# A hybrid decoder step on one core: the opening's products without the token's factor, six row tiles, shared decays

## The chip, the core and the metric

The kernel runs on one core of a Trainium2 chip. TensorE (PE) multiplies matrices into accumulators in PSUM; VectorE (DVE), ScalarE (ACT) and GpSimd (POOL) work on tiles of up to 128 partitions in SBUF, and VectorE and ScalarE also read the accumulators; SyncE (SP) issues most loads. The metric is device time in microseconds of one execution, as the median of several runs.

## What is computed

One inference step of a decoder layer for a prompt of 512 tokens and for 8 sequences of 8 sample tokens, 576 tokens in all, width 1024. The part that the change touches is the layer's input side:

```python
sh1, sc1, g1, sh2, sc2, g2 = split(silu(c) @ ada_w + ada_b, 6)      # per sequence and feature
hn = rmsnorm(x, norm1_w) * (1 + sc1) + sh1                          # rmsnorm: x * rsqrt(mean(x*x) + eps) * w
u = hn @ w_in                                                       # z, xbc, dt, q, k, v, o, ig, fg, xr, gr
xbc = silu(causal_conv(xbc, ...))                                   # width 4, with a state for the samples
y, ssm = ssd_chunked(xs, dt, a, bm, cm, s0)                         # decay = exp(cum[t] - cum[s]), masked
```

Behind it come an mLSTM and an RG-LRU on other columns of `u`, the output projection, and an MLP. The token's factor is the rsqrt: one number per token, the same for all features.

## The kernel before

Features lie on partitions, in 8 tiles (`KT`) of 128; tokens lie along the free axis, 512 of the prompt (`TP`) and 64 of the samples (`TS`), in two halves of 288 (`HALF`). A product block is 128 columns of a weight by 1024 features. Weights and activations are each split into a high and a low part in a reduced type (`w_prep`: ScalarE copies `wh`, L150, VectorE subtracts for `wl`, L151), and `mm_k` (L163) does three products by two halves, 6 matmuls for a feature tile, 48 for a block. A block accumulates in a pair of PSUM banks `g`; the pool behind `PG` has two such pairs, so a block's first matmul waits until the block before the last one has been copied out.

The opening, `start`, is written in the order in which each engine runs it (`in_order`). SyncE issues 8 loads of `x`, a vector of constants, and 8 column groups of `ada_w` (`ada`, 4 loads each, L354) with weight blocks between. The squares of `x` are summed over features by TensorE (`ms`, L271), raised to -1/2 on GpSimd (`rstd_cols`), and spread over partitions by transposes and a copy (`rstd_bcast`, tile `rb`). For each feature tile k, a column group of `ada_w` gives shift and scale: `ada_mm` (L217, row copy L219) and `ada_sel` (two transposes L227, a reduction L229 and an addition L231 on VectorE). `modulate` makes the tile's normalised `hnh` and `hnl` from `x`, `rb` and the scale `amp` (L292 to L303). The products of blocks 1 to 3 follow tile by tile, a step after their tile is there; `warm` puts filling matmuls between.

Blocks 1, 2 and 3 belong to the convolutions 8, 10 and 0. After them come the gates' products (`gates_mm`, L430, on the normalised `x`), and then block 4 and all later ones through `unit`, which issues a block's products, evicts, and calls `slot` twice; each `slot` advances the generators that run beside (gate rows, SSD, mLSTM, LRU, the later ada groups) by a step.

A convolution's eviction (`ev_conv`, `conv`) uses two row tiles of a ring, `R`, of 4: rows `r` and the sum `a`. GpSimd fills the left edges (L610, L611), ScalarE copies the accumulator in three pieces (L612, L614, L615) and starts the sum (L621), VectorE adds three taps (L627), ScalarE takes a tanh (L650), and VectorE makes `xbc` (L652, L654). The SSD's generator prepares a chunk's operands in `front` (the decay E: four Relu steps, L710, then an Exp, on each half of the heads) and uses them in `back`.

Of the kernel before, what the change touches and what calls it, by code (L numbers as in the profile page):

```python
# [22 lines left out]
FT = mybir.dt.float32  # L23
FR = mybir.dt.float32r
# [7 lines left out]
NT = TP + TS  # L32
# [35 lines left out]
class Kernel:  # L68
# [24 lines left out]
    def R(self):  # L93
        return self.rpool.tile([128, 608], FT, name=self.name("r"), tag="r")
# [27 lines left out]
    def w_load(self, upto):  # L122
        while self.w_next_dma <= min(upto, NBLK - 1):
            b = self.w_next_dma
            t = self.T("wg") if b == 0 else self.wpool.tile([128, 1024], FT, name=self.name("raw"), tag="raw", bufs=RAW_BUFS)
            src = self.io["wg"] if b == 0 else self.io["w"][b - 1]
            n = src.shape[1]
            self.nc.sync.dma_start(t[:, :n], src)
            self.w_raw[b] = t[:, :n].rearrange("p (k m) -> p k m", k=8)
            self.w_next_dma += 1  # L130

# [155 lines left out]
    def modulate(self, x, rb, k):  # L287

        nc = self.nc
        amp = self.rpool.tile([128, 9], FT, name=self.name("amp"), tag="amp", bufs=3)  # L290
        sc, sh = self.mod("sc1", k), self.mod("sh1", k)
        nc.vector.tensor_scalar(amp, sc, 1.0, self.v("nw1")[:, k:k + 1], op0=OP.add, op1=OP.mult)  # L292
        p, s = x[:, :TP], x[:, TP:].rearrange("p (b t) -> p b t", b=NB)
        nc.vector.scalar_tensor_tensor(p, p, amp[:, 0:1], rb[:, :TP], op0=OP.mult, op1=OP.mult)
        nc.gpsimd.tensor_tensor(x[:, TP:], x[:, TP:], rb[:, TP:], op=OP.mult)
        nc.gpsimd.tensor_tensor(s, s, amp[:, 1:, None].to_broadcast([128, NB, 8]), op=OP.mult)
        nc.gpsimd.tensor_tensor(s, s, sh[:, 1:, None].to_broadcast([128, NB, 8]), op=OP.add)
        hi, lo = self.T("hnh", FR), self.T("hnl", FR)
        nc.scalar.activation(hi[:, :TP], p, AF.Identity, bias=sh[:, 0:1])
        nc.scalar.activation(hi[:, TP:], x[:, TP:], AF.Copy)  # L300
        nc.vector.scalar_tensor_tensor(lo[:, :TP], p, sh[:, 0:1], hi[:, :TP].bitcast(FT), op0=OP.add, op1=OP.subtract)  # L301
        nc.gpsimd.tensor_tensor(lo[:, TP:], x[:, TP:], hi[:, TP:].bitcast(FT), op=OP.subtract)
        nc.gpsimd.tensor_scalar(p, p, sh[:, 0:1], None, op0=OP.add)  # L303
        return hi, lo
# [24 lines left out]
    def start(self):  # L329
# [6 lines left out]
        with self.in_order():  # L336
            x = [self.T("x") for _ in range(KT)]
            for k in range(KT):
                nc.sync.dma_start(x[k], io["x"][:, k])
# [10 lines left out]

            def load(q):
                ada[q] = [self.T("ada") for _ in range(4)]
                for i in range(4):
                    nc.sync.dma_start(ada[q][i][:, :512], io["ada"][q, :, i * 512:(i + 1) * 512])  # L354

            for q in range(PAIR_AT):
                load(q)
                self.w_load(W_AT.get(q, 0))
            ms = self.P("ms")
            self.warm(WARM[0])  # L360
            for k in range(0, KT, 2):
                sa, sb = self.R()[:, :NT], self.R()[:, :NT]
                nc.scalar.activation(sa, x[k], AF.Square)
                if k:
                    nc.vector.tensor_tensor(sb, x[k + 1], x[k + 1], op=OP.mult)
                else:
                    nc.scalar.activation(sb, x[k + 1], AF.Square)
                nc.vector.tensor_tensor(sb, sa, sb, op=OP.add)
                self.sum_tokens(sb, ms, k == 0, k == KT - 2)
                if k < KT - 2:  # L370
                    self.warm(WARM[1])
            th = self.rpool.tile([128, 8, 32], FT, name="cth", tag="r")
# [3 lines left out]
            rows = {}  # L376

            def ada_mm(q):
                t = ada.pop(q)
                rows[q] = self.ada_mm(lambda k: t[k // 2][:, (k % 2) * 256:(k % 2 + 1) * 256])  # L380

            ada_mm(0)
            self.w_prep(0)
            for q in range(PAIR_AT, KT):
                if q == VEC_AT:
                    nc.sync.dma_start(self.vec[:, NV1:], io["vec"][:, NV1:])
                load(q)
                self.w_load(W_AT.get(q, 0))
            self.w_load(4)
            self.start_dma = self.last()  # L390
            rb = self.rstd_bcast(r)
            self.warm(WARM[2])
            self.ada_sel(0, rows[0])
            self.hn = [None] * KT
            self.hn[0] = self.modulate(x[0], rb, 0)
            self.w_prep(1)
            self.warm(WARM[3])
            ada_mm(1)
            self.ada_sel(1, rows[1])
            ada_mm(2)  # L400
            pgs = [self.PG(), self.PG(), PairTile(banks=[self.P("g"), self.P("g")])]
            for k in range(KT):
                if k + 1 < KT:
                    self.hn[k + 1] = self.modulate(x[k + 1], rb, k + 1)
# [1252 lines left out]
```

## Time and profile before

| | us |
|---|---|
| median of 3 runs (lowest, highest) | 977.28 (972.36, 979.8) |
| the profiled execution | 978.69 |
| its span, from the first to the last instruction | 976.9 |
| block 4's first matmul starts | 62.08 |
| block 5's, block 6's | 70.09, 76.44 |

The span is some 2 us shorter than the time of the same execution, since the time has the launch in it. In the page and in the answers of the trace a row of a group gives line, engine, operation, out<-in with the program's names, shape and number, then busy time and the mean of one in ns, then the engine's idle time before them and what ended it. A timeline's row gives start, duration, engine, line and tile, and in brackets the idle time before it and who ended it; a pair of halves is one row.

### The profile page before, as it was taken

To read this page: it belongs to the slowest core of one execution; us is meant where nothing else is said; L and a number is where in the kernel's file an instruction comes from. 1 tells how busy PE (TensorE), PEld (TensorE's weight loads), DVE (VectorE), ACT (ScalarE), POOL (GpSimd) and SP (SyncE) were. 2 spreads that over 40 slices of the span, in tenths; PEclk is the share of its full clock that TensorE was granted. 3 is DMA by queue.
4 is the path that set the end of the run, shared out by engine and by line. 5 is a ranking of instruction groups with operands and counts; after the bars stand their busy time and mean duration, and the time that the engine had idled before them with its cause. 6 is when DMAs were issued, how large, how long until landed. Compare 5 with 4: busy or idle time off the path is not lost.

```text
span 976.9 us, 18063 instructions
## 1 busy us (share of the span) xinstructions
PE 952.2 (97%) x7322; PEld 897.4 (92%) x7322; DVE 572.0 (59%) x1166; ACT 417.4 (43%) x805; POOL 136.8 (14%) x194
## 2 busy tenths in 40 slices
PE   8999899999999899999999999999999999999996
PEld 4689888888888899998999999999999999999996
DVE  3769887686885594666444456433553355335544
ACT  3356786485765664554222244312331243114321
POOL 1821213302441221110000000000000000000032
PEclk8999999999999999999999999999999999999998
DMA  9712275656633435333333222222222222222202
GB/s 345 302 66 87 76 209 179 228 164 189 219 130 122 153 110 176 120 128 124 111 111 109 80 87 86 71 82 88 87 87 74 79 87 87 87 77 76 87 23 97
DMA packets 51218, 119.61 MB, mean 122 GB/s; under 512 B 6956, under 2 KB 17468, under 8 KB 51136
## 3 DMA queue, kind: packets, MB, share of 16 engines
q1 hardware_dynamic: 47024, 111.06, 33.5%
q10 hardware_dynamic: 3744, 6.85, 1.8%
q8 instruction: 58, 0.95, 0.4%
q0 software_dynamic: 368, 0.55, 0.2%
q14 instruction: 24, 0.20, 0.1%
HBM read 108.68 MB, written 9.76 MB: 121 GB/s over the span
## 4 chain that ended last, share of the span: by engine, by line
PE 86%; DVE 3%; ACT 2%; DMA 1%; issue 1%; SPq 0%; POOL 0%; POOLq 0%; ACTq 0%; DVEq 0%
PE g L163 75%; PE adap L217 1%; PE g L1382 1%; DMA cumb<-scr_cum 1%; PE ps L742 1%; PE py L737 1%; PE pc L840 1%; PE lg L1148 1%; PE py L740 1%; DMA ada<-ada 1%; PE pu L847 0%; ACT att L710 0%; PE pu L997 0%; PE pn L989 0%; DVE wl L151 0%
## 5 line engine op out<-in xcount | busy, mean ns | idle before, releaser
L150 ACT ACTIVATE wh<-raw 128x1024 fp32r<-128x1024 f32 x123 | 130.0, 1058 | 348.1 <-PE g L163 326.9
L151 DVE TENSOR_TENSOR wl<-raw,wh 128x1024 fp32r<-128x1024 f32 x123 | 152.2, 1238 | 48.2 <-ACT wh L150 42.3
L163 PE MATMUL g<-hnh,wh 128*128 128x288 f32 x688 | 155.0, 305 | 8.8 <-ACT r L615 5.2
L163 PE MATMUL g<-hnh,wl 128*128 128x288 f32 x688 | 153.3, 302 | 0.3 <-DVE wl L151 0.3
L163 PE MATMUL g<-hnl,wh 128*128 128x288 f32 x688 | 151.5, 299 | 0.2 <-DVE hnl L301 0.2
L163 PEld LDWEIGHTS g<-hnh,wh 128*128 128x128 f32 x688 | 111.7, 190 | 17.4 <-ACT r L615 6.1
L163 PEld LDWEIGHTS g<-hnh,wl 128*128 128x128 f32 x688 | 111.7, 190 | 4.3 <-issue 3.1
L163 PEld LDWEIGHTS g<-hnl,wh 128*128 128x128 f32 x688 | 112.1, 190 | 2.6 <-issue 1.6
L163 PE MATMUL g<-h2h,wh 128*128 128x288 f32 (+1 forms) x512 | 111.2, 298 | 0.0
L163 PE MATMUL g<-h2l,wh 128*128 128x288 f32 (+1 forms) x512 | 110.9, 298 | 0.0
L163 PE MATMUL g<-h2h,wl 128*128 128x288 f32 (+1 forms) x512 | 110.4, 297 | 0.0
L163 PE MATMUL g<-hh,wh 128*128 128x288 f32 x480 | 102.7, 295 | 0.0
L163 PE MATMUL g<-hh,wl 128*128 128x288 f32 x480 | 102.6, 295 | 0.0
L163 PE MATMUL g<-hl,wh 128*128 128x288 f32 x480 | 102.4, 295 | 0.0
L308 DVE SCALAR_TENSOR_TENSOR xr<-g,modt,xr 128x288 f32<-128x288 f32 x38 | 19.7, 518 | 140.9 <-PE g L163 140.9
L163 PEld LDWEIGHTS g<-h2h,wl 128*128 128x128 f32 x512 | 83.7, 189 | 0.0
L163 PEld LDWEIGHTS g<-h2l,wh 128*128 128x128 f32 x512 | 83.5, 189 | 0.0
L163 PEld LDWEIGHTS g<-h2h,wh 128*128 128x128 f32 x512 | 83.4, 189 | 0.1
L163 PEld LDWEIGHTS g<-hl,wh 128*128 128x128 f32 x480 | 77.1, 188 | 0.0
L163 PEld LDWEIGHTS g<-hh,wh 128*128 128x128 f32 x480 | 76.9, 188 | 0.0
L163 PEld LDWEIGHTS g<-hh,wl 128*128 128x128 f32 x480 | 76.8, 188 | 0.0
L1424 POOL TENSOR_SCALAR xr<-xr,vec 128x576 f32<-128x576 f32 (+2 forms) x8 | 15.2, 1902 | 384.6 <-ACT sqa L1256 364.0
(399 smaller groups left out, 1527.3 us busy)
## 6 DMA issues: line engine op xcount, KB each, us to landing
raw<-w SPq DMA_DIRECT2D x124, 512.0 KB, 3.5
ada<-ada SPq DMA_DIRECT2D x32, 512.0 KB, 5.1
ada<-ada SPq DMA_DIRECT2D x32, 256.0 KB, 5.8
cumb<-scr_cum SPq DMA_DIRECT2D x16, 256.0 KB, 5.5
s<-s SPq DMA_DIRECT2D x16, 256.0 KB, 4.4
ssm_s<-s ACTq DMA_DIRECT2D x16, 256.0 KB, 4.8
x<-x SPq DMA_DIRECT2D x8, 288.0 KB, 5.3
xr<-x SPq DMA_DIRECT2D x8, 288.0 KB, 3.9
```

Of the source, the lines that this page charges most:

```text
L150: nc.scalar.activation(hi, raw, AF.Copy)
L151: nc.vector.tensor_tensor(lo, raw, hi.bitcast(FT), op=OP.subtract)
L163: self.nc.tensor.matmul(pg.h[h][:m, :e], w(k), xx[:, h * HALF:h * HALF + e], start=start and n == 0, stop=stop and n == 2)
L217: nc.tensor.matmul(ps[32 * j:32 * j + 32, :256], self.cs[:, k, :], ks(k), start=k < 4, stop=k >= 4)
L308: self.nc.vector.scalar_tensor_tensor(dst[:, :HALF], pg.h[0][:, :HALF], gate[:, 0:1], x[:, :HALF], op0=OP.mult, op1=OP.add)
L737: nc.tensor.matmul(o, xdt[:, h * 64:(h + 1) * 64], att[h // 4][:, hs], start=True, stop=not c)
L740: nc.tensor.matmul(o, S[:, h * 64:(h + 1) * 64], ce[h // 4][:, hs], start=False, stop=True)
L742: nc.tensor.matmul(pst, cb[:, 128:256], xend[:, :512], start=True, stop=True)
L840: nc.tensor.matmul(pc[32 * j:32 * j + 32, :], Cc[:, TP + 32 * q:TP + 32 * q + 32], s0[4 * q + j][:, :512], start=True, stop=True)
L1148: nc.tensor.matmul(ps[hh][:, :HALF], self.lw[w // 4][:, w % 4 * 128:(w % 4 + 1) * 128], x[:, hh * HALF:(hh + 1) * HALF], start=True, stop= ...
L1382: nc.tensor.matmul(pgs[i].h[p][:, :c.stop - c.start], w(k), xs[k][x][:, c], start=k == 0 and j == 0, stop=k == 7 and j == 2)
L1424: self.eng("fin").tensor_scalar(x, x, self.v("fnw")[:, o:o + 1], None, op0=OP.mult)
```

## The change

It has five parts.

1. Blocks 1 to 3 are multiplied by `x` times the scale without the token's factor (`scale_only`: `hxh`, `hxl`; ten columns more in the second half carry the shift). The factor is applied when the accumulator is emptied: `late_rows` multiplies the rows by `rb1` on VectorE and adds the product of the shift. The sum of squares stands behind the products of the first four tiles. The full normalised tiles are still made, by `modulate` in three steps `a`, `b`, `c`, for the blocks from 4 on and the gates. Block 4 and the gates' products move into `start`: four tiles of block 4, the gates, the other four. The gates' product gets the shift as a column.
2. The loads of `x`, `ada` and weights are interleaved by a list, `LOADS`, and the filling matmuls are set anew.
3. The ring `R` has 6 row tiles, not 4; two of `late_rows`' results take the place of `r`.
4. In the SSD's `front` the first half of the heads has its decay by VectorE (subtract, minimum), the second half still by ScalarE.
5. The generator of the SSD waits a slot more ahead of the first chunk's `back`, and in the samples' part the second of two stacks is made later.

TensorE's queue around the sum of squares, before (`ms` the sum, `adap` an ada group's product, `ba` and `bb` the broadcast, `r` and `col` the squares and the factor):

```order
L271 MATMUL ms_136<-ones,r_198 128x1 x4
L271 MATMUL ms_136<-ones,r_198 64x1
L217 MATMUL adap_216<-ada_106,cs 32x256 x2
L217 MATMUL adap_216<-ada_107,cs 32x256 x2
L217 MATMUL adap_216<-ada_108,cs 32x256 x2
L217 MATMUL adap_216<-ada_109,cs 32x256 x2
L279 MATMUL ba_272<-vec,col_214 128x128 x4
L281 MATMUL bb_273<-vec,col_214 128x64
```

and in the changed kernel, from the transposes of group 5 on (`g_205` is block 2's accumulator, `hxh_463` tile 4's unfactored high part):

```order
L229 MATMUL adas_519<-vec,adarow_511 128x128 x2
L165 MATMUL g_205<-hxh_463,wh_299 128x288
L165 MATMUL g_205<-hxh_463,wh_299 128x298
L165 MATMUL g_205<-hxl_464,wh_299 128x288
L165 MATMUL g_205<-hxl_464,wh_299 128x298
L165 MATMUL g_205<-hxh_463,wl_300 128x288
L165 MATMUL g_205<-hxh_463,wl_300 128x298
L281 MATMUL ba_543<-vec,col_494 128x128 x4
L283 MATMUL bb_544<-vec,col_494 128x64
```

The broadcast stood behind the sum and one ada product ahead of all products; now it stands behind five tiles of blocks 1 and 2, and the sum itself behind four tiles of both.

VectorE's queue ahead of block 4, before (`gs`, `gv` are the gates, `cwh` the taps' weights):

```order
L294 SCALAR_TENSOR_TENSOR x_90<-x_90,amp_626,rb_279 128x512
L301 SCALAR_TENSOR_TENSOR hnl_633<-x_90,modt,hnh_632 128x512
L151 TENSOR_TENSOR wl_640<-raw_270,wh_639 128x1024
L151 TENSOR_TENSOR wl_781<-raw_772,wh_780 128x1024
L151 TENSOR_TENSOR wl_785<-raw_774,wh_784 128x1024
L433 COPY gs_709<-gp_691 128x288
```

and in the changed kernel (`g_204` is block 1's accumulator, `r_737` its late rows):

```order
L328 SCALAR_TENSOR_TENSOR hnl_637<-x_86,modt,hnh_636 128x512
L316 SCALAR_TENSOR_TENSOR x_88<-x_88,amp_118_525,rb_550 128x512
L328 SCALAR_TENSOR_TENSOR hnl_688<-x_87,modt,hnh_687 128x512
L316 SCALAR_TENSOR_TENSOR x_89<-x_89,amp_133_594,rb_550 128x512
L336 COPY shw_738<-g_204 128x9
L339 TENSOR_TENSOR r_737<-g_204,rb_550 128x288
L340 TENSOR_TENSOR r_737<-g_204,rb_550 128x224
L341 TENSOR_TENSOR r_737<-g_204,rb_550 128x8x8
L344 TENSOR_TENSOR r_737<-r_737,shw_738 128x8x8
L328 SCALAR_TENSOR_TENSOR hnl_708<-x_88,modt,hnh_707 128x512
```

The late rows of block 1, which free the accumulator that block 4 takes, stand behind the tiles' normalising steps on VectorE, where ScalarE emptied that accumulator before.

ScalarE's queue at the eviction of block 4, before (`r_843` are its rows, `g_771` its accumulator):

```order
L650 ACTIVATE r_739<-r_745 128x600
L612 ACTIVATE r_755<-g_347 128x288
L614 ACTIVATE r_755<-g_348 128x224
L615 ACTIVATE r_755<-g_348 128x8x8
L621 ACTIVATE r_761<-r_755,cwh 128x600
L612 ACTIVATE r_843<-g_771 128x288
L614 ACTIVATE r_843<-g_771 128x224
```

and in the changed kernel (`r_913`, `g_763`):

```order
L763 ACTIVATE r_737<-r_871 128x600
L734 ACTIVATE r_903<-r_893,cwh 128x600
L589 ACTIVATE ic_859<-gp_788,gp 4x288
L589 ACTIVATE ic_859<-gp_789,gp 4x224
L152 ACTIVATE wh_1017<-raw_823 128x1024
L725 ACTIVATE r_913<-g_763 128x288
L727 ACTIVATE r_913<-g_763 128x224
```

Block 4's rows still come behind those of blocks 1 to 3, and they are the seventh row tile: the ring gives them the tile of block 1's rows, after that block's last step on VectorE.

The diff, cut to its core:

```diff
-        return self.rpool.tile([128, 608], FT, name=self.name("r"), tag="r")
+        return self.rpool.tile([128, 608], FT, name=self.name("r"), tag="r", bufs=6)
+    def scale_only(self, x, k):
+        nc.vector.tensor_scalar(amp, self.mod("sc1", k), 1.0, self.v("nw1")[:, k:k + 1], op0=OP.add, op1=OP.mult)
...
+        nc.gpsimd.tensor_copy(u[:, TS:TS + 9], self.mod("sh1", k))
+        nc.gpsimd.memset(u[:, TS + 9:], 0.0)
...
+        nc.scalar.activation(hi[:, :TP], x[:, :TP], AF.Copy, scale=amp[:, 0:1])
+        nc.scalar.activation(hi[:, TP:n], u, AF.Copy)
+        nc.vector.scalar_tensor_tensor(lo[:, :TP], x[:, :TP], amp[:, 0:1], hi[:, :TP].bitcast(FT),
+                                       op0=OP.mult, op1=OP.subtract)
+        nc.vector.tensor_tensor(lo[:, TP:n], u, hi[:, TP:n].bitcast(FT), op=OP.subtract)
+    def modulate(self, step, x, k, u, amp):
+        if step == "a":
+            nc.vector.scalar_tensor_tensor(p, p, amp[:, 0:1], rb[:, :TP], op0=OP.mult, op1=OP.mult)
+            nc.gpsimd.tensor_tensor(s, u[:, :TS], rb[:, TP:], op=OP.mult)
...
+        if step == "b":
+            nc.scalar.activation(hi[:, :TP], p, AF.Identity, bias=sh[:, 0:1])
+            nc.scalar.activation(hi[:, TP:], s, AF.Copy)
+        else:
+            nc.vector.scalar_tensor_tensor(lo[:, :TP], p, sh[:, 0:1], hi[:, :TP].bitcast(FT), op0=OP.add, op1=OP.subtract)
+            nc.gpsimd.tensor_tensor(lo[:, TP:], s, hi[:, TP:].bitcast(FT), op=OP.subtract)
+    def late_rows(self, pg):
+        r = self.R()
+        nc.vector.tensor_copy(sh, pg.h[1][:, HALF:HALF + 9])
...
+        nc.vector.tensor_tensor(r[:, 3:3 + HALF], pg.h[0][:, :HALF], self.rb1[:, :HALF], op=OP.mult)
+        nc.vector.tensor_tensor(r[:, 3 + HALF:515], pg.h[1][:, :n], self.rb1[:, HALF:TP], op=OP.mult)
...
+        nc.scalar.activation(r[:, 3:515], r[:, 3:515], AF.Identity, bias=sh[:, 0:1])
+        nc.vector.tensor_tensor(s, s, sh[:, 1:, None].to_broadcast([128, NB, 8]), op=OP.add)
@@ start
+            mm(0, 3)
+            mm(1, 3)
+            ms = self.P("ms")
+            self.sum_tokens(sqa, ms, True, True)
             r = self.rstd_cols(ms, 1.0 / D, EPS)
...
+            mm(1, 4)
+            self.rb1 = self.rstd_bcast(r)
+            mm(2, 4)
+            whole(("a", 0), ("a", 1))
...
+            for i in range(3):
+                mm(i, 7)
+            whole(("b", 4), ("c", 4), ("a", 6))
+            r0 = self.late_rows(pgs[0])
+            whole(("b", 5), ("c", 5), ("a", 7), ("b", 6), ("c", 6), ("b", 7), ("c", 7))
+            pg = self.PG()
+            for k in range(4):
+                self.mm_k(pg, 4, k, self.hn[k], k == 0, False)
+            ps, g = self.gates_mm(x)
+            r1 = self.late_rows(pgs[1])
...
+            for k in range(4, KT):
+                self.mm_k(pg, 4, k, self.hn[k], False, k == KT - 1)
+                if k == 5:
+                    self.gates_sel(ps, g)
             self.ev_gates(ps)
+        self.ev_conv(pgs[0], 8, r0)
+        self.ev_conv(pgs[1], 10, r1)
+        self.ev_conv(pgs[2], 0, self.late_rows(pgs[2]))
+        self.ev_conv(pg, 1)
@@ ssd, front
+                    if h2:
+                        nc.scalar.activation(e, cum, AF.Relu, scale=-1.0, bias=col)
+                    else:
+                        nc.vector.tensor_scalar(e, cum, col, 0.0, op0=OP.subtract, op1=OP.min)
+                nc.scalar.activation(E[:, :512], E[:, :512], AF.Exp, scale=-1.0 if h2 else 1.0)
@@ ssd, over the chunks
+            if c == 0:
+                yield
@@ constants
-WARM = 14, 4, 4, 6
-PAIR_AT = 3
-W_AT = {0: 1, 2: 2, 4: 3}
+WARM = 18, 3, 8, 4, 8
+LOADS = [(t[0], int(t[1:] or 0)) for t in "x0 x1 q0 w1 q1 x2 w2 x3 q2 x4 w3 x5 q3 x6 x7 q4 q5 w0 q6 v q7 w4".split()]
```

More of the change, by code (lines that the diff above doesn't have):

```diff
@@ L372, in start @@
-            th = self.rpool.tile([128, 8, 32], FT, name="cth", tag="r")
+            for what, i in LOADS:
+                if what == "x":
+                    nc.sync.dma_start(x[i][:, :NT], io["x"][:, i])
+                elif what == "q":
+                    ada[i] = [self.T("ada") for _ in range(4)]
+                    for j in range(4):
+                        nc.sync.dma_start(ada[i][j][:, :512], io["ada"][i, :, j * 512:(j + 1) * 512])
+                elif what == "w":
+                    self.w_dma(i)
+                else:
+                    nc.sync.dma_start(self.vec[:, NV1:], io["vec"][:, NV1:])
@@ L373, in start @@
+            self.w_next_dma = 5
+            self.start_dma = self.last()
+            self.w_prep(0)
+            self.warm(WARM[0])
+            th = self.rpool.tile([128, 8, 32], FT, name="cth", tag="r", bufs=6)
             nc.scalar.activation(th, ct, AF.Tanh, scale=0.5)
             nc.vector.scalar_tensor_tensor(self.cs, th, 1.0, ct, op0=OP.add, op1=OP.mult)
-            r = self.rstd_cols(ms, 1.0 / D, EPS)
[L376 to L395, printed above, removed]
@@ L416, in start, with ada_mm, sel @@
-            if not GATES_FIRST:
-                ps = self.gates_mm(x)
+            rows, amps, early, xs = {}, {}, {}, {}
+            sqa = self.T("sqa")[:, :NT]
+            def ada_mm(q):
+                if q < KT:
+                    t = ada.pop(q)
+                    rows[q] = self.ada_mm(lambda k: t[k // 2][:, (k % 2) * 256:(k % 2 + 1) * 256])
+            def sel(q):
+                if q < KT:
+                    self.ada_sel(q, rows.pop(q))
+                    early[q], amps[q], xs[q] = self.scale_only(x[q], q)
@@ new lines, in square, with mm @@
+            def square(k):
+                if k == 0:
+                    nc.scalar.activation(sqa, x[0][:, :NT], AF.Square)
+                else:
+                    t = self.R()[:, :NT]
+                    nc.scalar.activation(t, x[k][:, :NT], AF.Square)
+                    nc.vector.tensor_tensor(sqa, sqa, t, op=OP.add)
+            pgs = [self.PG(), self.PG()]
+            def mm(i, k):
+                self.mm_k(pgs[i], 1 + i, k, early[k], k == 0, k == KT - 1, NSH)
+            self.hn = [None] * KT
@@ new lines, in whole @@
+            def whole(*steps):
+                for step, k in steps:
+                    self.modulate(step, x[k], k, xs[k], amps[k])
+            ada_mm(0)
+            self.warm(WARM[1])
+            sel(0)
+            self.w_prep(1)
+            square(0)
+            square(1)
+            self.warm(WARM[2])
+            mm(0, 0)
+            ada_mm(1)
+            self.warm(WARM[3])
+            sel(1)
+            square(2)
+            self.w_prep(2)
+            self.warm(WARM[4])
+            mm(0, 1)
@@ new lines, in start @@
+            ada_mm(2)
+            mm(1, 0)
+            sel(2)
+            square(3)
+            mm(1, 1)
+            self.w_prep(3)
+            mm(0, 2)
+            ada_mm(3)
+            mm(1, 2)
+            square(4)
+            sel(3)
+            square(5)
+            pgs.append(PairTile(banks=[self.P("g"), self.P("g")]))
+            mm(2, 0)
+            mm(2, 1)
+            ada_mm(4)
+            square(6)
+            mm(2, 2)
+            sel(4)
+            square(7)
+            mm(0, 3)
@@ L1303, in inp @@
             blk += 1
-        for i in range(1, 4):
+        for i in range(2, 4):
             inp(lambda pg: self.ev_conv(pg, i))
```

184 lines of the change are left out of this document (88 added, 96 removed).

## The prediction, made before the changed kernel ran

> **What bounds the kernel now.** I read the page first: the sum of each engine, then the chain that ended last.
>
> ```profile
> span 976.9 us, 18063 instructions
> PE 952.2 (97%) x7322; PEld 897.4 (92%) x7322; DVE 572.0 (59%) x1166; ACT 417.4 (43%) x805; POOL 136.8 (14%) x194
> PE 86%; DVE 3%; ACT 2%; DMA 1%; issue 1%; SPq 0%; POOL 0%; POOLq 0%; ACTq 0%; DVEq 0%
> ```
>
> TensorE is busy for 952.2 of 976.9 us, and most of that is products that the change keeps. Something can be won only where TensorE waits, runs at a low clock, or does filling work, and that is the opening. So the second view is busy time by stretch, cut at the opening's landmarks.
>
> ```profile
> core 0: us, PE busy (x) PEld busy (x) DVE busy (x) ACT busy (x) POOL busy (x), PEclk, DMA share, GB/s
> 20.00:29.50 9.50, 7.70 (x79) 4.23 (x81) 6.90 (x15) 3.72 (x8) 6.34 (x9) 1.00 1.04 397
> 32.91:36.32 3.41, 3.13 (x14) 2.77 (x13) 2.44 (x6) 0.87 (x2) 2.23 (x5) 0.50 1.03 383
> 36.32:56.50 20.18, 20.18 (x175) 17.78 (x174) 13.80 (x26) 8.86 (x16) 15.45 (x24) 1.00 0.43 160
> 56.50:62.08 5.58, 3.37 (x37) 1.50 (x36) 2.72 (x5) 2.18 (x6) 0.00 (x0) 1.00 0.57 193
> 62.08:70.10 8.02, 8.02 (x49) 8.02 (x50) 5.54 (x8) 3.22 (x7) 0.87 (x6) 0.79 0.00 0
> 70.10:101.70 31.60, 31.60 (x242) 31.60 (x240) 29.32 (x46) 19.23 (x37) 5.89 (x19) 1.00 0.24 84
> 120.00:160.00 40.00, 39.32 (x350) 33.35 (x349) 34.52 (x70) 29.41 (x73) 7.59 (x9) 1.00 0.68 204
> ```
>
> Up to 36 us the loads run at 383 to 397 GB/s and TensorE follows them. From 36.3 to 56.5 it is busy throughout: what lies there can't get shorter by better supply. From 70 to 102 VectorE is busy 29.32 of 31.60 us, so there it is nearly a second bound. Third, the waits and the timeline of TensorE say what its idle time is.
>
> ```profile
> PE g L163 <- ACT r L615: 5.2, 3, 2.1
> PE g L163 <- ACT k L920: 0.9, 1, 0.9
> 62.08 0.54 PE L163 MATMUL g<-hnh,wh 128*128 128x288 f32 x2 [2.09 <-ACT r L615]
> 70.09 0.43 PE L163 MATMUL g<-hnh,wh 128*128 128x288 f32 x2
> 76.44 0.42 PE L163 MATMUL g<-hnh,wh 128*128 128x288 f32 x2
> 103.52 0.53 PE L163 MATMUL g<-hnh,wh 128*128 128x288 f32 x2 [1.55 <-ACT r L615]
> 112.25 0.53 PE L163 MATMUL g<-hnh,wh 128*128 128x288 f32 x2 [1.56 <-ACT r L615]
> ```
>
> These are first matmuls of blocks 4, 5, 6, 10 and 11. An undisturbed block takes 76.44 - 70.09 = 6.35 us, 0.79 per feature tile. Three blocks wait for the copy L615 that empties an accumulator: 5.2 us together, all that this view offers the change besides 0.9 at L920.
>
> **The change, part by part**, as times at landmarks after it.
>
> *The token factor.* Its square sum now stands behind products that need ada column group 4, so I start from the loads.
>
> ```profile
> DMA to landing us min/median/max: 5.3/5.8/7.1
> 30.92 2.31 SPq L354 DMA_DIRECT2D ada<-ada  x4
> 13.63 2.00 PE L271 MATMUL ms<-ones,r 128*128 128x1 f32 x10
> 17.43 1.12 PE L279 MATMUL ba<-vec,col 128*128 128x128 f32 x4
> 36.83 0.38 PE L227 MATMUL adas<-vec,adarow 128*128 128x128 f32 x2
> 37.14 1.07 PE L217 MATMUL adap<-ada,cs 128*32 128x256 f32 x16
> L363 ACT ACTIVATE r<-x 128x576 f32<-128x576 f32 x4 | 2.7, 683 | 5.6 <-DMA x<-x 2.1 <-DVE r L368 1.9 <-DVE r L365 1.6
> L368 DVE TENSOR_TENSOR r<-r,r 128x576 f32<-128x576 f32 x4 | 3.0, 757 | 4.2 <-ACT r L367 4.0
> L299 ACT ACTIVATE hnh<-x,modt 128x512 fp32r<-128x512 f32 x8 | 5.8, 723 | 14.1 <-DVE x L294 14.1
> ```
>
> The last ada load is issued by 33.2 and lands some 5.8 later, at about 38.7; the new list moves the same bytes. Behind group 4 it has groups 5, 6 and 7 (1.05 MB each) and some 0.5 MB more, 3.65 MB, 9.2 us at 397 GB/s: group 4 lands at 29.4. Its product (1.0), its row copy behind a square (0.4) and its transposes (0.4) end at 31.6 with the queueing. VectorE's two square additions (0.76 each) and the three small selection steps bring 33.0; ScalarE's scaled copy, its tail and the last square (0.72, 0.25, 0.68) bring 34.6; the last addition 35.4. TensorE, which has no product left ahead of that sum, is idle for about 2.5 us here. Then the sum (half of 2.00, the row's four sums in ten), three products of 0.79, one ada product 1.07, transposes 0.38, the broadcast (1.12 and 0.2) and its copy 0.6: the factor is ready at 42.0. The power on GpSimd lies beside those products.
>
> *VectorE up to the late rows.* From there its queue is fixed: twelve steps on whole tiles, two selections, a weight split, a wait, and the rows of block 1 from the accumulator.
>
> ```profile
> L294 DVE SCALAR_TENSOR_TENSOR x<-x,amp,rb 128x512 f32<-128x512 f32 x8 | 6.2, 770 | 0.4
> L301 DVE SCALAR_TENSOR_TENSOR hnl<-x,modt,hnh 128x512 fp32r<-128x512 f32 x8 | 6.4, 794 | 6.3 <-ACT hnh L299 6.3
> L292 DVE TENSOR_SCALAR amp<-modt,vec 128x9 f32<-128x9 f32 x8 | 2.8, 353 | 0.6
> L151 DVE TENSOR_TENSOR wl<-raw,wh 128x1024 fp32r<-128x1024 f32 x13 | 16.2, 1250 | 6.4 <-ACT wh L150 6.1
> L308 DVE SCALAR_TENSOR_TENSOR xr<-g,modt,xr 128x288 f32<-128x288 f32 x38 | 19.7, 518 | 140.9 <-PE g L163 140.9
> L654 DVE SCALAR_TENSOR_TENSOR xbc<-r,r 128x64 f32<-128x64 f32 x10 | 2.2, 220 | 0.0
> L303 POOL TENSOR_SCALAR x<-x,modt 128x512 f32<-128x512 f32 x8 | 13.5, 1685 | 0.0
> ```
>
> Twelve times 0.78 is 9.4. A selection is 0.35 for the scale, 0.79 for the low part and four small ones of some 0.2, 2.0 each, 4.0 for two; the split 1.25; waits for ScalarE I put at 0.7. The products of an accumulator with a row of factors are shown nowhere; nearest are 0.52 at L308, which also reads an accumulator, and 0.22 for 64 columns: 0.52 + 0.42 + 0.22 = 1.2 for the first rows. Sum 16.55, to 58.5. Bounds: without waits and 0.1 less per step (GpSimd no longer runs L303's 13.5 us beside them) 56.5; with each step a quarter longer 62.5. TensorE has its three blocks done at about 54 and idles 4.5 us.
>
> The Trainium skill, "GPSIMD Engine Reference", section 8, says that GpSimd shares its memory interfaces with VectorE and contends with VectorE steps of two SBUF inputs. By it alone the twelve steps would take the lower bound, and the late rows end near 57; the new small GpSimd steps per tile take some of that back. I keep the means.
>
> *Block 4 and the gates move into the opening.* Block 4's accumulator is block 1's, so it starts at 58.5. Its work is 8 × 0.79 and the gate products inside it.
>
> ```profile
> 56.51 2.15 PE L430 MATMUL gp<-x,wg 128*32 128x288 f32 x32
> L627 DVE SCALAR_TENSOR_TENSOR r<-r,cwh,r 128x600 f32<-128x600 f32 x32 | 26.2, 836 | 4.5 <-ACT r L621 4.2
> L652 DVE SCALAR_TENSOR_TENSOR xbc<-r,r 128x512 f32<-128x512 f32 x10 | 6.8, 683 | 0.1
> L612 ACT ACTIVATE r<-g 128x288 f32<-128x288 f32 x11 | 4.4, 402 | 2.0 <-DVE xbc L654 1.9
> L710 ACT ACTIVATE att<-cumb,col 128x128 f32<-128x128 f32 x8 | 2.4, 391 | 0.0
> L574 DVE TENSOR_SCALAR it<-mx,mt 4x128 f32<-4x128 f32 x3 | 0.8, 272 | 0.0
> ```
>
> 6.35 + 2.15 + 0.6 for the selection is 9.1. Before's block 4 takes 8.02 instead of 6.35 at a granted clock of 0.79, after an idle of 2.09; an idle of 4.5 should cost no less, so I add the same 1.7. Block 5 starts at 69.3, against 70.1.
>
> *Block 6 is where VectorE binds.* VectorE waits for the gates (65.5 with the low clock). Behind that wait stand the gate copy (0.5, as L308), rows of blocks 2 and 3 (2 × 1.2 and four small steps, 0.6), six taps (5.0), three weight splits (3.75), gate rows (1.2) and block 1's last conv step (0.9): 14.2 us, to 79.7. Only then is a row tile free for block 4's eviction: six tiles are already used by blocks 1 to 3. The eviction takes 1.0 (L612 and its two companions), and block 6, which needs that accumulator, starts at 80.7 instead of 76.4: 4.3 us lost. Bounds: 2.3 lost if the late rows come at 56.5, 8.3 if at 62.5.
>
> *Six row tiles.* They let two more evictions run ahead of VectorE. I give them both later stalls, 1.55 + 1.56 = 3.1 us won; at the other end nothing, if VectorE has fallen too far behind.
>
> *Decays shared, one slot more.* Thirty-two steps of 0.39 (L710) leave ScalarE, thirty-two of some 0.27 (nearest: L574, also 128 columns) come on VectorE, eight fronts of four. ScalarE's help is worth at most the wait at L920, 0.9. On VectorE, busy 34.52 of 40 us from 120 to 160, they cost nothing if they fit and 4 × 1.1 = 4.3 if the first group's four fronts all lie on the path. I take 0.9 won, since TensorE's waits there are mostly ScalarE's. The extra slot and the deferred sample stacks only shift work under a busy TensorE; with that cover gone they would cost under 1.
>
> *Extra columns.* Ten in 298 of the second half of each pair, 72 pairs: by the rate of a pair, 576 columns in 0.79 / 3 = 0.26 us, 72 × 10 columns are 0.3 us, ahead of an idle TensorE, so nothing.
>
> Sum: + 4.3 - 3.1 - 0.9 = + 0.3. Against its own time of 978.69 that is 979.0. That execution lies 1.4 above the median of the three runs, 977.28; against the median I get 977.5.
>
> **Rivals.** *The opening gets through (faster, 965).* My weakest landmark is group 4 at 29.4: a load is 5.8 us in flight, so groups overlap by 5.8 × 397 GB/s = 2.3 MB, and it could be whole up to 4 us sooner. With no step queued ahead of its hops (1.5 less) the factor comes at 36.5; with VectorE at its lower rate (12 × 0.67, 2 × 1.6, 1.23 and 1.0 are 13.5) late rows come at 50. TensorE's own work, 24 × 0.79 and eight ada products with their transposes, 1.45 each, sum and broadcast 2.4, is 33 us and also ends at about 50 if it starts at 17; it doesn't idle and keeps its clock. Gates at 50 + 3.2 + 2.15 = 55.3, VectorE's list at the same lower rate 11.6, eviction 1.0: block 6 at 68, 8.4 early; with 3.1 and 0.9 the gain is 12.4, 965 from the median. It makes the one per cent if block 6 starts before 70.6. For it: L303's 13.5 us vanish, and VectorE has only 13.80 of 20.18 us in use now. Against: both gifts are needed at once.
>
> *VectorE falls a block behind (slower, 988).* VectorE's queue waits at each selection for the round trip over all engines: product 1.07, row copy 0.4, transposes 0.4, selection 0.8, scaled copy 1.0, low part 0.8, each with about 0.2 of handing over, 5.5. If each of the last three selections (tiles 5 to 7) stops the queue for 5.5 instead of 2.0, late rows come 10.5 late, at 69.0, and block 6 at 91.2: 0.3 + 10.5 = 10.8 slower, 988. It passes one per cent once the late rows come after 68 (after 65 if the ring doesn't help). Against: before's chain has the same hops, and TensorE is busy all through 36 to 56.
>
> *The ring doesn't help (980.5):* the two stalls stay since VectorE, not tile count, holds the evictions: 3.1 more.
>
> *The clock (979 or 976).* Before has a half-clock window of 3.41 us at 32.91, and its block 4 ran low after an idle of 2.09; the new idle of 2.5 at 33 could bring one more, which delays the factor by up to 1.7: 979. The Trainium skill, "TensorE: Matmul & The Clock Gate", Part 1, says half rate comes only after an idle window of about 3.4 us, free-running. By it the 2.5 need bring none, and the 4.5 only if it covers a window: 976 without the 1.7. The low clock after 2.09 speaks against reading it that strictly.
>
> **Chances.** The forecast 0.40, ring 0.10, clock 0.13; the opening through 0.23; VectorE behind 0.14. One per cent is 9.8 us, about what a measurement here can tell from no change: faster 0.23, same 0.63, slower 0.14. The forecast's own bounds are 975.6 (2.3 - 3.1 - 0.9) and, if all bad ends fell together, 989.9 (8.3 + 0 + 4.3), of which I take 986 as the usual end. The range goes from 962, the faster rival's 965 and 3 us for its unsure hops, to 987; it leaves out most of the slower rival and the far end of the faster, under 2 in 10.
>
> **What would show it.** TensorE idle ahead of the square sum, waiting for VectorE's last addition, and again ahead of block 4, waiting for the factor products; block 6 waiting for ScalarE's eviction, and that for block 1's last conv step; the two 1.55 us stalls gone. If block 4 starts before 52 or block 6 before 71, the faster rival holds; if block 6 starts after 86, the slower. I am wrong altogether if TensorE's busy time itself changes by more than 3 us after 120, where I moved only small steps.

## The result: slower by 3.8 per cent, and the profile after

| | before | changed |
|---|---|---|
| median | 974.93 us (4 runs, 972.36 to 979.8) | 1011.94 us (4 runs, 1010.92 to 1014.09) |
| ratio | | 1.0376, 95% interval 1.0326 to 1.0427 |
| profiled execution, span | 976.9 us | 1009.9 us |

The changed kernel takes 37 us more; the profiled pair differs by 33.0 us of span. The kernel before ran in two groups (972.4 and 972.6 us, and 977.3 and 979.8), and its profiled execution, at 978.69, is of the second, which makes the 4 us between the two figures. The changed kernel's page, the span, the sum of each engine and the chain that ended last:

```profile
span 1009.9 us, 18079 instructions
PE 962.0 (95%) x7296; PEld 902.0 (89%) x7297; DVE 588.3 (58%) x1240; ACT 417.5 (41%) x787; POOL 124.9 (12%) x202
PE 78%; DMA 8%; DVE 7%; ACT 4%; issue 2%; SPq 1%; POOL 0%; POOLq 0%; DVEq 0%; ACTq 0%
```

TensorE is busy 9.8 us longer, for nearly the same products, and idle for the other 23 us, and DMA's share of the chain goes from 1% to 8%. To see where, I compared the starts of the product blocks, each read from the timeline as the first matmul of the block (us from the span's start):

| block | before | changed | later by |
|---|---|---|---|
| 4 | 62.1 | 61.9 | -0.2 |
| 6 | 76.4 | 82.2 | 5.8 |
| 9 | 95.5 | 102.9 | 7.5 |
| 13 | 128.1 | 131.6 | 3.5 |
| 16 | 166.7 | 180.4 | 13.7 |
| 24 | 268.2 | 293.5 | 25.3 |
| 32 | 344.0 | 374.0 | 30.0 |
| 122 | 945.5 | 976.9 | 31.4 |

The opening itself, which the prediction worked through, ends 3.5 us late at block 13. The next 26.5 us are lost between blocks 13 and 32, where the SSD, the mLSTM and the gates' later work run beside the products; behind block 32 the two kernels run nearly alike (1.4 us more up to block 122). Busy time from block 13's start to block 32's, in the kernel before and then in the changed one (PE's busy time first, its granted clock third from the end):

```profile
128.12:344.04 215.92, 211.43 (x1722) 183.33 (x1720) 156.50 (x381) 140.03 (x352) 59.44 (x67) 1.00 0.54 174
```

```profile
131.63:374.03 242.40, 220.60 (x1736) 189.84 (x1737) 167.67 (x425) 139.72 (x337) 55.52 (x69) 0.96 0.49 158
```

TensorE's idle time goes from 4.5 us to 21.8, 17.3 more, and its busy time from 211.4 to 220.6, 9.2 more; together that is the 26.5. In the changed kernel the clock is at half in three parts of this stretch:

```profile
144.63:154.87 10.24, 5.84 (x24) 5.78 (x24) 4.77 (x11) 4.84 (x12) 0.00 (x0) 0.50 0.69 234
219.72:223.14 3.42, 2.95 (x10) 0.91 (x10) 2.82 (x14) 1.82 (x6) 0.00 (x0) 0.50 1.04 415
291.40:298.23 6.83, 6.07 (x22) 5.07 (x23) 5.89 (x22) 2.22 (x4) 0.20 (x2) 0.50 0.85 287
```

TensorE is busy for 14.86 us of them, so the clock makes at most 7.4 (half of that) of the 9.2 us. No other engine is full (VectorE is busy for 167.7 of 242.4 us): the engines wait for each other. The changed kernel's waits of TensorE, the longest first:

```profile
PE g L165 <- ACT q L1042: 6.9, 1, 6.9
PE g L165 <- ACT r L728: 4.3, 3, 2.5
PE g L165 <- DVE r L341: 4.2, 1, 4.2
PE pu L968 <- ACT kt L1073: 3.3, 1, 3.3
PE ms L273 <- DVE col L259: 2.3, 1, 2.3
```

The longest, at 142 us, can be followed through four queues. ScalarE's timeline shows why the copy `q` is late:

```profile
146.38 0.98 ACT L825 ACTIVATE att<-cumb,col 128x128 f32<-128x128 f32 x3 [4.82 <-DMA cumb<-scr_cum]
148.34 0.63 ACT L1042 ACTIVATE q<-g 128x576 f32<-128x576 f32 x1
```

It stands behind a decay step of the SSD that waits for a load of the cumulative sums. SyncE's timeline has that load behind another, which reads the gate rows' ends:

```profile
139.13 0.33 SPq L703 DMA_DIRECT2D decb<-scr_ends  x1
139.51 0.98 SPq L781 DMA_DIRECT2D cumb<-scr_cum  x2
```

And GpSimd's timelines show when the gate rows store their sums and their ends, in the kernel before and in the changed one:

```profile
101.23 0.74 POOL L525 DMA_DIRECT2D scr_cum<-cum  x1 [5.56 <-DVE cum L520]
118.08 0.54 POOL L589 DMA_DIRECT2D scr_ends<-ends  x1 [0.36 <-ACT ends L585]
```

```profile
119.51 0.74 POOL L637 DMA_DIRECT2D scr_cum<-cum  x1 [6.11 <-DVE cum L632]
135.93 0.54 POOL L701 DMA_DIRECT2D scr_ends<-ends  x1 [2.35 <-ACT ends L697]
```

Both come 18 us later, while the products of the same time are 3.5 us late. That lag is the thing to explain.

### The profile page after: what moved, and what is told of

The parts are those of the page before. It is cut to its first block, busy times and chain, and to the rows that moved or that the text cites. A ratio compares the mean times of both kernels' runs of the same rounds, so it can differ in the third digit from the quotient of the medians.

```text
span 1009.9 us, 18079 instructions
## 1 busy us (share of the span) xinstructions
PE 962.0 (95%) x7296; PEld 902.0 (89%) x7297; DVE 588.3 (58%) x1240; ACT 417.5 (41%) x787; POOL 124.9 (12%) x202
## 4 chain that ended last, share of the span: by engine, by line
PE 78%; DMA 8%; DVE 7%; ACT 4%; issue 2%; SPq 1%; POOL 0%; POOLq 0%; DVEq 0%; ACTq 0%
PE g L165 69%; DMA ada<-ada 2%; DMA x<-x 1%; DVE wl L153 1%; PE adap L219 1%; PE g L1504 1%; DMA cumb<-scr_cum 1%; DMA s<-s 1%; DMA c<-c 1%; DMA nmb<-scr_nm 1%; ACT wh L152 1%; PE lg L1270 1%; DVE r L740 1%; PE py L853 1%; DMA cumf<-scr_cum 0%
## 5 line engine op out<-in xcount | busy, mean ns | idle before, releaser
L165 PE MATMUL g<-hnh,wh 128*128 128x288 f32 x656 | 150.0, 309 | 16.8 <-ACT q L1042 6.9
L165 PE MATMUL g<-hnh,wl 128*128 128x288 f32 x656 | 147.6, 303 | 0.0
L165 PE MATMUL g<-hnl,wh 128*128 128x288 f32 x656 | 147.6, 304 | 0.0
L165 PEld LDWEIGHTS g<-hnh,wh 128*128 128x128 f32 x656 | 108.5, 194 | 25.0 <-issue 8.1
L165 PEld LDWEIGHTS g<-hnh,wl 128*128 128x128 f32 x656 | 109.1, 193 | 3.2 <-issue 2.7
L165 PEld LDWEIGHTS g<-hnl,wh 128*128 128x128 f32 x656 | 108.9, 193 | 1.7 <-issue 1.3
L165 PE MATMUL g<-hh,wh 128*128 128x288 f32 x480 | 102.9, 296 | 0.0
L349 DVE SCALAR_TENSOR_TENSOR xr<-g,modt,xr 128x288 f32<-128x288 f32 x38 | 19.7, 517 | 142.0 <-PE g L165 142.0
```

The source lines that it names most:

```text
L165: self.nc.tensor.matmul(pg.h[h][:m, :e], w(k), xx[:, h * HALF:h * HALF + e], start=start and n == 0, stop=stop and n == 2)
L349: self.nc.vector.scalar_tensor_tensor(dst[:, :HALF], pg.h[0][:, :HALF], gate[:, 0:1], x[:, :HALF], op0=OP.mult, op1=OP.add)
```

## The experiments

Each kernel was compared with runs of the kernel before on the same chip. "Stretch" is the time from block 13's start to block 32's, in its profile; it is 215.9 us before and 242.4 in the changed kernel. The changed kernel itself was timed only in the first session, and before's median lay between 974.93 and 981.16 us from one session to the next. What an edit wins is therefore read from the stretch, and from the time above before's of the same session. The first theory (A) was that the gate rows stand too late, the second (B) that the SSD's own edits cost the time. A third (C) came with later experiments: the fixed order of the queues fits the old arrival of the SSD's inputs, and any shift costs.

**Which half of the change.** The opening alone undoes the ring, the slot, the decays and the stacks:

```diff
-        return self.rpool.tile([128, 608], FT, name=self.name("r"), tag="r", bufs=6)
+        return self.rpool.tile([128, 608], FT, name=self.name("r"), tag="r", bufs=4)
...
-                    if h2:
+                    if True:
...
-            if c == 0:
-                yield
...
         stack(0)
+        stack(1)
```

> The changed kernel with only its opening changed: four row tiles and 54 tiles as before, all decays on ScalarE, no extra slot, both sample stacks made together as before. Theory A (the gate rows start a block later in the order, so the SSD's loads and products stand badly in the fixed queues from 128 to 320 us): some 20 to 35 us slower than before remain, block 12 within 6 us of before. Theory B (the SSD's own edits cost it): within 5 us of before.

It took 1001.88 us, 1.0223 of before (1.0161 to 1.0284): 20.7 us slower, as theory A said. But block 12 starts 12.5 us later (131.2 against 118.7), not within 6. Of its 21.8 us at block 32, 11.1 are there at block 13 already and 10.7 come in the stretch, which is 226.6. The rest alone, put into the kernel before:

> The kernel before with all of the change but its opening: six row tiles, 53 tiles, half the decays on VectorE, a slot more, the second stack later. Theory A: 0 to 4 us faster than before, since the two waits of 1.55 us go. Theory B: 20 to 30 us slower than before.

989.48 us, 1.0104 (1.0067 to 1.0142): 8.3 us slower, where A said 0 to 4 faster and B 20 to 30 slower. So both halves cost, the opening the more, and neither theory is right alone. The rest alone is even 7.1 us earlier at block 13 and loses 17 us behind it.

**One part taken from the changed kernel.** Without the extra slot:

```diff
-            if c == 0:
-                yield
             S = back(c, S, ready.pop(0))
```

> The changed kernel without the extra slot ahead of the first chunk's products. Theory A: the loss stays within 8 us of the changed kernel's, to either side. If the slot itself makes the loss (part of theory B), at least 15 us of the 37 come back.

999.49 us; its stretch is 230.8, so 11.6 of the 26.5 us are gone. With all decays on ScalarE:

```diff
-                    if h2:
+                    if True:
                         nc.scalar.activation(e, cum, AF.Relu, scale=-1.0, bias=col)
```

> The changed kernel with all decays on ScalarE again. Theory A: within 8 us of the changed kernel. If VectorE's 32 more steps make the loss, at least 15 us come back.

1002.59 us, stretch 234.3, 8.1 gone. Against before of the same session these two kernels are 18.3 and 21.4 us slower, so 18.7 and 15.6 of the 37 have come back; by their own times it is 12.5 and 9.4. Both are more than theory A's 8, but whether the 15 us of the other mark came back depends on which of the two counts. Both edits together:

> The changed kernel without the extra slot and with all decays on ScalarE. If the two parts cost on their own (12 and 8 us of the stretch from block 13 to block 32 when each is taken away alone), some 6 us of that stretch's 26.5 remain and the time is 8 to 14 us above before. If each is only another order that happens to fit or not (theory C: the fixed queues of the SSD's stretch fit the old arrival of its inputs, and any shift costs), the two gains don't add: 10 to 20 us of the stretch remain.

997.94 us, 22.2 above before; stretch 230.1: 12.3 gone, not 19.7, and 14.2 remain. The two don't add, as theory C said: what each takes away is for the most part the same loss. And the slot put alone into the kernel before:

> The kernel before with the extra slot alone. If the slot costs wherever it stands: 8 to 14 us slower. If it costs only together with the late gate rows: within 4 us of before.

981.42 us, 1.0055 (1.0029 to 1.0082), 5.7 us slower, between the two marks; stretch 222.7. There the slot costs 6.8 us of the stretch, against 11.6 in the changed kernel.

**One link of the long wait.** The load of the ends goes to GpSimd's queue, so that the sums don't wait behind it:

```diff
-        nc.sync.dma_start(self.decb, bcast(self.scr_ends, 0, [[1, 36 * 12]]))
+        nc.gpsimd.dma_start(self.decb, bcast(self.scr_ends, 0, [[1, 36 * 12]]))
```

> The changed kernel with one load, that of the chunk-end decays, issued by GpSimd behind its own store instead of by SyncE. If that load holds the next cumulative sums up (issued at 139.5 behind it, though their own source is there since 122), ScalarE's wait of 4.8 us and TensorE's of 6.9 near 142 us shrink by 3 us or more, and the time falls 4 to 10 us. If the sums are late for another reason: no change within 3 us.

SyncE's timeline and TensorE's waits of this kernel:

```profile
135.42 0.98 SPq L781 DMA_DIRECT2D cumb<-scr_cum  x2
```

```profile
PE pu L968 <- ACT kt L1073: 3.8, 1, 3.8
PE g L165 <- ACT q L1042: 2.4, 1, 2.4
```

The sums are issued 4.1 us earlier, ScalarE no longer waits for them, and the wait for `q` falls from 6.9 to 2.4, as the chain says; but the time is 1009.34 us, 2.6 below the changed kernel's, and not 4 to 10. Up to block 29 it is 4.1 us ahead (347.4 against 351.5). That block then runs partly at half clock and takes 2.4 us longer, in this kernel and then in the changed one:

```profile
347.41:357.38 9.97, 9.97 (x66) 9.22 (x65) 3.71 (x8) 3.16 (x6) 1.98 (x1) 0.73 0.25 90
```

```profile
351.48:359.04 7.56, 7.56 (x65) 6.81 (x65) 3.70 (x8) 3.17 (x6) 1.98 (x1) 1.00 0.36 121
```

At block 32 1.7 us are left. Even the 4.1 are a small part of the 30.0: this wait, however well explained, isn't the main cause.

**The gate rows earlier or later in the order.** A step of their generator is given two slots sooner in the changed kernel, with and without the extra slot, and with the SSD as before and six row tiles; and two slots later in the kernel before:

```diff
         self.start()
+        self.slot()
+        self.slot()
         blk = 5
```

> The changed kernel with the gate rows' generator advanced two steps ahead of block 5, as many as it had before. Theory A (the gate rows, and with them the whole SSD, stand one block too late in the order): 12 us or more of the 33 to 37 come back, and the 6.87 us wait of TensorE near 142 us goes. Rival (VectorE is behind after the opening, and two more steps burden it more): within 5 us of the changed kernel, or slower.

> The same without the extra slot ahead of the first chunk's products. Theory A: block 32 at most 12 us later than before. Rival: as slow as the changed kernel without that slot, some 18 us slower than before, or slower.

> The changed opening with six row tiles and the gate rows two steps earlier, everything in the SSD as before. Theory A: the stretch from block 13 to block 32 loses under 6 us, and the time is within 8 us of before. Theory C: it still loses 8 us or more there.

> The kernel before, its opening untouched, with the gate rows' generator two slots (one block) later. Theory A: 10 to 25 us slower, all of it between blocks 13 and 32. Rival (it is VectorE's lateness from the opening): under 4 us slower.

1002.67, 996.33, 1001.68 and 981.56 us; stretches 233.7, 223.4, 228.2 and 229.6. In the first the wait for `q` falls from 6.9 to 0.6 us, and 12.5 us of the 37 come back against before (9.3 by its own time), about theory A's 12; but block 13 comes 4.1 us later in exchange. In the second block 32 is 17.2 us later than before, not at most 12, and the time is 18.2 us above before's, which was the rival's mark. The third loses 12.3 us in the stretch, not under 6, which was theory C's mark. The fourth is slower by only 0.4% (0.9972 to 1.0107), the rival's mark again; but its gate rows' last store came only 0.9 us later, so it decides little. The ring alone on the kernel before:

> The kernel before with six row tiles and 53 tiles and nothing else. If the ring takes the two waits of 1.55 us: block 13 some 3 us earlier and the time 0 to 4 us shorter. If any shift of the order in the SSD's stretch costs time: up to 10 us slower by block 32 although block 13 is earlier.

982.19 us, 1.0045 (1.0017 to 1.0072), stretch 228.3: 11.1 us early at block 13 and no earlier at block 32. Of the 11.1 us 4.0 are not the ring's: block 4 starts at 58.05 in this profile, though its opening has the same steps as before's (the last section has more on this).

**A regularity.** Over these fourteen kernels the stretch runs from 215.9 to 242.4 us. But counted from the gate rows' last store (`scr_ends`), block 32 starts at much the same distance:

| kernel | ends stored | block 13 | block 32 | from ends to 32 |
|---|---|---|---|---|
| before | 118.1 | 128.1 | 344.0 | 226.0 |
| before_ring6 | 115.8 | 117.0 | 345.3 | 229.5 |
| before_gates_late2 | 119.0 | 119.3 | 348.9 | 229.9 |
| open_only | 136.3 | 139.2 | 365.8 | 229.5 |
| no_extra_slot | 137.3 | 133.0 | 363.8 | 226.5 |
| no_slot_decays_act | 136.5 | 132.2 | 362.3 | 225.8 |
| slots2_no_extra | 136.1 | 137.8 | 361.2 | 225.1 |
| opening_ring6_slots2 | 133.3 | 135.0 | 363.3 | 230.0 |
| decays_act (slot) | 135.9 | 131.6 | 365.9 | 230.0 |
| before_slot (slot) | 112.5 | 122.5 | 345.2 | 232.7 |
| mid_only (slot) | 119.8 | 121.0 | 354.2 | 234.4 |
| slots2 (slot) | 133.9 | 135.7 | 369.4 | 235.5 |
| decb_on_pool (slot) | 136.1 | 131.8 | 372.4 | 236.2 |
| changed kernel (slot) | 135.9 | 131.6 | 374.0 | 238.1 |

In the eight kernels without the extra slot it is 225 to 230 us, in the six with it 230 to 238. Theory A became: the gate rows' end sets block 32, and the products set it only where they are later still. Two kernels test it by moving the gate rows far, six slots late in the kernel before and six steps early in the changed one (without the extra slot):

```diff
+        yield
+        yield
+        yield
+        yield
+        yield
+        yield
         sp = self.T("sp")
         for _ in self.softplus([(slice(64 * h, 64 * h + 64), sp[:64, h * HALF:(h + 1) * HALF]) for h in range(2)],
```

> The kernel before with the gate rows' generator six slots (three blocks) later. If the end of the gate rows sets block 32 (theory A, as sharpened): that store comes 8 us or more later than before's 118, block 32 follows it by 224 to 232 us, and the time is 8 to 25 us longer. If the products set it: block 32 stays within 8 us of before's 344, since blocks 5 to 13 don't come later.

994.94 us, 1.0175 (1.0065 to 1.0285). GpSimd's timeline of it:

```profile
128.87 0.54 POOL L595 DMA_DIRECT2D scr_ends<-ends  x1 [3.97 <-ACT ends L591]
```

It comes 10.8 us later than before's. Block 13 starts at 117.6, 10.6 us earlier than before's, and block 32 at 358.3, 14.3 later: 229.4 us behind the store, as theory A said. An untouched opening, early products and late gate rows give about half of what the changed kernel lost: 14.3 of 30.0 us at block 32, 17.2 us of time.

> The changed kernel without the extra slot, the gate rows advanced six steps ahead of block 5. Theory A: the store that ends the gate rows comes 4 us or more ahead of 137, though block 13 comes later than 133 since VectorE does the convolutions later; block 32 follows the store by 224 to 232 us, so it starts earlier than 364. If the products set it: block 32 comes later than 364 by as much as block 13.

1000.01 us. The store comes at 125.3, 12 us sooner, but block 32 at 362.3 is only 1.5 us sooner:

```profile
125.34 0.54 POOL L701 DMA_DIRECT2D scr_ends<-ends  x1
```

```profile
PE ca L709 <- DVE cs L654: 6.7, 1, 6.7
PE g L165 <- ACT r L728: 6.2, 2, 3.6
```

Now the convolutions are late: TensorE waits 6.7 us for the gate rows and 6.2 for evictions, block 13 starts at 151.0, 18.0 us later than without the six steps, and from there to block 32 it takes 211.3 us, less than before's 215.9. Neither mark is met in full: block 32 is 237.0 us behind the store, not 224 to 232, and it isn't later than 364 either. That the products set it here fits the 211.3, the shortest of all, but isn't shown. In none of the variants of the changed kernel did both the gate rows and the products come early.

**Three attempts at a better kernel.** The kernel before with six row tiles and the gate rows two, four and one steps earlier; of the edit, the slots for two steps:

```diff
         self.start()
+        self.slot()
+        self.slot()
         blk = 4
```

> The kernel before with six row tiles and the gate rows two steps earlier, nothing else. Theory A: the store that ends them comes at 106 to 114 (115.8 with the ring alone), and the time is 2 to 8 us below before's. If the products set it: the same as the ring alone, 0 to 5 us above before.

> The same with four steps. Theory A: the store another 1 to 4 us earlier, and the time no longer than with two steps by more than 2 us. If the products set it: slower than with two steps, since the convolutions wait.

> The kernel before with six row tiles and the gate rows one step earlier. If block 32 starts at the later of 226 to 230 us after the gate rows' end and 211 to 217 us after block 13: the end lies between those with no step (115.8) and two steps (111.1), block 13 between 117 and 125, and block 32 at 338 to 344; the time is 0 to 6 us below before's. If the ring is worth nothing with any step: 0 to 4 us above.

975.97 us (0.9985, 0.9954 to 1.0016), 981.54 (1.0059, 1.0024 to 1.0093) and 974.68 (0.9976, 0.9951 to 1.0001). The stores come at 111.1, 108.3 and 114.6, block 32 at 339.7, 343.1 and 337.2. With two steps the store comes as theory A said, but the time is 1.8 us below before's and not 2 to 8. With four it is 5.6 us above that, not at most 2, which was the other theory's mark. With one step the time is 2.8 us below before's, as expected, but block 32 lies just ahead of the expected 338, only 222.6 us behind the store. None of the three is measurably faster than before. But with two steps and with one, block 32 is 5.6 and 8.1 us earlier than with the ring alone (345.3).

## Why the prediction was wrong

*The opening, right in kind, some 3 us late.* TensorE waits 2.3 us ahead of the square sum (2.5 forecast) and 4.2 ahead of block 4 (4.5). Block 6 waits for ScalarE's eviction, and that for block 1's last conv step, as said:

```profile
61.89 0.50 PE L165 MATMUL g<-hnh,wh 128*128 128x288 f32 x2 [4.20 <-DVE r L341]
73.09 0.43 PE L165 MATMUL g<-hnh,wh 128*128 128x288 f32 x2
82.20 0.53 PE L165 MATMUL g<-hnh,wh 128*128 128x288 f32 x2 [2.55 <-ACT r L728]
81.37 0.41 ACT L725 ACTIVATE r<-g 128x288 f32<-128x288 f32 x1 [0.88 <-DVE xbc L767]
```

Block 4 at 61.9 was forecast for 58.5, block 5 at 73.1 for 69.3, block 6 at 82.2 for 80.7. The 3.4 us at block 4 arise ahead of the factor, which is ready at 45.3 and not at 42.0: the square sum starts at 37.0 instead of 35.4, and behind its wait the clock falls to half:

```profile
38.82:42.23 3.41, 3.41 (x23) 1.86 (x22) 0.00 (x0) 0.39 (x1) 1.03 (x1) 0.50 1.03 413
```

From the factor to the late rows it takes 16.4 us (16.55 forecast). The two waits have nearly the forecast length since both of their ends came late, and block 6 is only 1.5 us off because VectorE's work behind the gates took 12.8 us (68.5 to 81.3) and not 14.2; so these small differences are partly luck. (The prediction's own list for that work adds up to 14.35, not 14.2. And its "all that this view offers" passed over waits of TensorE in the opening of the kernel before: 3.3 us for `adarow` and 1.9 for `wh`.) The ring takes the later stalls: from 7.5 us late at block 9 the kernel comes to 3.5 at block 13, 4.0 won where 3.1 was forecast. The sum of these terms was 1.2 late at block 13, and 3.5 came.

*The steps that failed* are two, and in place of the 0.9 us that they were to win the stretch behind the opening lost 26.5. The first is the one on the slot and the decays: "I take 0.9 won", and the extra slot and the deferred stacks "only shift work under a busy TensorE; with that cover gone they would cost under 1." Taken out together, slot and decays give 12.3 of the 26.5 back. The deferred stacks were not tested by themselves. The other 14.2 us remain without either, and go with a term that the prediction put at nothing: what the late gates do to the SSD. In that run (no_slot_decays_act) the gate rows' end is 18.4 us late and block 32 18.3. I read a TensorE busy for 39.32 of 40 us as cover. The reading that fits the runs is a balance: in the kernel before, block 32 comes 226.0 us behind the gate rows' end and 215.9 behind block 13, both near the lowest that any kernel reached (222.6 and 211.3).

*What I left out* was written down in the prediction itself: "VectorE waits for the gates (65.5 with the low clock)". That wait ends at 58.3 in the kernel before and at 68.5 in the changed one:

```profile
58.26 0.46 DVE L433 COPY gs<-gp 128x288 f32<-128x288 f32 x1 [0.83 <-PE gp L430]
99.58 1.34 DVE L520 TENSOR_TENSOR_SCAN cum<-rm,val 64x576 f32<-64x576 f32 x1
```

```profile
68.52 0.46 DVE L536 COPY gs<-gp 128x288 f32<-128x288 f32 x1 [2.48 <-PE gp L533]
117.86 1.34 DVE L632 TENSOR_TENSOR_SCAN cum<-rm,val 64x576 f32<-64x576 f32 x1
```

I asked what stood behind that wait for block 6 and not what stood behind it for the SSD. The 17.85 us by which the gate rows' end is late add up from the two traces: the gates' products start at 66.77 instead of 56.51, 10.26; from there to VectorE's scan of the sums (`cum`) it takes 51.09 us instead of 43.07, 8.02; and the steps from sums to ends take 0.43 less. In those 51.1 us VectorE does 27 convolution taps where it did 21, 5.0 us, and 9 weight splits where it did 5, 4.9 us. Six row tiles and the generator's later start each let some of the convolutions go first: with four row tiles (open_only) it is 24 taps and 8 splits in 48.6 us, with the two slots back (slots2) 24 and 8 in 47.2. But neither makes the lateness: their gate rows' ends still come at 136.3 and 133.9.

*The rest of the loss.* Block 32 is 30.0 late: 17.8 of it is the gate rows' end, and 12.1 the longer way from there, 238.1 instead of 226.0. Without the extra slot that way is 226.5, with all decays on ScalarE 230.0. So the 12.1 hang on slot and decays together; how they act together wasn't taken apart.

*The rivals.* The slower one had the right sign and engine, VectorE behind, but a place that was refuted by its own mark: late rows were done at 61.7, not after 68, and block 6 started before 86. The clock rival's new half clock did come, at 38.82 behind a wait of 2.3 us, with its 1.7 us inside the lateness of the factor. The ring did help: block 13 starts at 131.6 with it and at 139.2 with four row tiles (open_only). The lower bound for VectorE's twelve steps did not come: they took 0.78 to 0.80 us on the mean in the changed kernel, 0.77 and 0.79 before. The mark by which I would be "wrong altogether", TensorE's busy time changed by more than 3 us after 120, is met: from block 13's start to the end it is busy for 835.2 us before and 847.2 in the changed kernel. The lower clock behind the new waits may make up to 9.1 of these 12.0 us.

*What stays open.* That block 32 follows the gate rows' end by 225 to 230 us is a regularity of eight kernels without the extra slot, and held when the end was moved by 10.8 us in the kernel before. It isn't a law: of the later kernels two with other steps of the gate rows came at 234.8 and 237.0, with late convolutions, and one at 222.6. Between the ring alone and the ring with one step the store moved by 1.2 us and block 32 by 8.1, so the store's time is not all that counts. Which steps of the SSD and mLSTM make up those 226 us wasn't found, and moving the gate rows also moves the order of the queues, so that lateness (theory A) and order (theory C) weren't told apart fully.

## What to carry to other kernels

A stretch in which the first engine is full may be full because two chains end there at the same time; then work laid beside it need not be free, and each chain's first input is to be followed, not only the engine's waits. When a change moves the start of a side computation, look for its next store or load that others read, and compare that landmark with the products' landmarks: 18 us against 3.5 told here what no list of waits did. And taking one explained wait away (4.5 us of it here) may win only 1.7 us further on: a kernel in which the suspected input is moved far, with as little else as can be, says more on whether it sets the end.

## What the runs showed of the hardware

The same opening ran 4 us shorter in some profiles: block 4 starts at 62.08 in the kernel before and at 58.05 in the one with six row tiles, whose opening has the same steps. Busy time from 30 to 40 us, in the kernel before and then in the other:

```profile
30.00:40.00 10.00, 7.78 (x62) 6.18 (x54) 6.01 (x12) 4.18 (x9) 7.90 (x14) 0.83 1.03 393
```

```profile
30.00:40.00 10.00, 9.54 (x95) 7.17 (x94) 7.59 (x17) 3.55 (x8) 7.62 (x13) 1.00 1.04 397
```

The first has a stretch at half clock there and the second none. TensorE's longest wait just ahead is 1.94 us in the first and 1.09 in the second. The Trainium skill, "TensorE: Matmul & The Clock Gate", Part 1, has a free-running window of about 3.4 us, and the half clock "after ≥1 idle window". The first profile doesn't fit an idle window: its half clock starts at 32.91, and in the 3.41 us ahead of that TensorE is busy for 1.47:

```profile
29.50:32.91 3.41, 1.47 (x20) 0.81 (x20) 1.90 (x3) 2.20 (x4) 2.89 (x6) 1.00 1.05 393
```

In the changed kernel a wait of 2.27 us, ending at 37.04, was followed by half clock from 38.82. Whether the place of a wait in such a window decides what it costs isn't shown here, since the waits differ in length too.

The largest new wait, 6.9 us at 142 us, cost the clock as well. The half clock from 144.63 to 154.87, shown with the result, starts within it; TensorE was busy for 5.84 of those 10.24 us, so the half clock added up to 2.9 us to the wait itself.
